# A hybrid transformer block on one core: the sums of Strassen products continued in a PSUM bank, and twenty splits moved from GpSimd to VectorE

## The chip, the cores and the metric

The kernel runs on one core of a Trainium2 chip. The metric is the device time of one execution in microseconds. The engines are called as in the profile: PE is TensorE's matmul, DVE is VectorE, ACT is ScalarE, POOL is GpSimd, SP is SyncE, which here issues DMAs. PSUM is the memory that PE writes; a bank holds 128 x 512 float32.

## The reference

One block over x of 1024 rows by 1024 columns. What the change touches is the projection into q, k and the gates, and the first matmul of the feed-forward part:

```python
h_in = rms_norm(x, norm_mix_g[l], NORM_EPS)
proj = h_in @ w_in[l]
qa, ka, va, qb, kb, vb, ga, gb = jnp.split(proj, split_idx, axis=-1)
...
merged = jax.nn.sigmoid(ga) * ya + jax.nn.sigmoid(gb) * yb
x = x + merged @ w_out[l]
h2 = rms_norm(x, norm_mlp_g[l], NORM_EPS)
x = x + jnp.square(jax.nn.relu(h2 @ w_ff1[l])) @ w_ff2[l]
return rms_norm(x, norm_final_g, NORM_EPS)
```

Between the two stand a windowed attention with three dilations and a differential attention, each with rotary positions on q and k.

## The kernel before

The program is one straight list of instructions, written as Python with tiles taken from pools. A scheduler puts it into an order for each engine; on the chip each engine then works through its own queue in that order, and semaphores make it wait for others. A tile's tag has a number of buffers ("slots"), and a new tile of the tag must wait until the readers of the tile that had its slot before are done.

The execution has five stages: norm and v (0 to 144 us), q, k and gates (144 to 426 us), attention, the branch outputs, the output projection and the early part of ff1 (426 to 1057 us), ff1 (1057 to 1327 us) and ff2 (1327 to 1700 us).

In the second and fourth stage a block of 256 output columns, a *pair*, is computed as two halves by the seven products of Strassen and Winograd. There are 8 q/k pairs, 8 gate pairs and 16 ff1 pairs. The transposed activations lie ready as seven operands named B11, B21, B22, T1, T2, T3 and T4. A product (L242) is twelve matmuls of 128 x 128 by 128 x 512: four steps of K by three terms, since each float32 operand is split into a high part (`_h`, written by ACT) and a low part (`_l`, the rest, a subtraction on POOL or DVE). The split is `halves` (L248); its tiles `wh` and `wl` have three slots each.

Of each pair come these steps. `col_raw` loads two tiles of weights, `w_n0` and `w_n1`, 512 KB each, by SP; raw tiles have two slots for each of two turns, so that the load for a pair takes the slot of the pair two before. `rest_operands` (L270) makes four sums on DVE: `s` (L273), and in place a21 (L274), a11 (L275) and a12 (L276); then the splits `ws` (of a11 and a12, for T2 and B22), `wd` (of `s`, for T1) and `wt` (of a21 and a22, for T3 and T4). `ws` and `wt` are split by POOL, 128 x 1024 each, `wd` by DVE. `rest_products` (L282) issues the five products T2, B22, T1, T3 and T4 into five banks: two double banks with the tag S (names `y...` and `z...`) and one with the tag T (`4...`), all with two slots. Six sums on DVE make the blocks c12, c22 and c21 out of the banks. The pair's other two products, B11 and B21, give `p1` and c11 in `first_products` (L262); `w1a` and `wa` are the splits for them.

These two come at different times. Four of the q/k pairs (EARLY) and seven of the ff1 pairs have p1 beforehand; the other four q/k pairs and ff1 pairs 7 to 13 compute it in their own turn, so they have seven products; the gates and ff1 pairs 14 and 15 leave it out here (`p1 is None`) and add it later. So the second stage has 88 products and the fourth 94. The order of the ff1 pairs is 6, 0, 1, 2, 3, 4, 5, 7 and up. In the second stage q/k pairs and gates alternate, and each q/k pair is followed by its rotary step (`rope`, L496 to L515): four DMAs, one multiplication on POOL (L503), three instructions on DVE (L502, L504, L513) of 128 x 1024, and one on ACT.

In the functions below `done` stores a finished block; in ff1 ACT first squares it (`squared`, L1140).

Of the kernel before, what the change touches and what calls it, by code (L numbers as in the profile page):

```python
# [19 lines left out]
P = 128  # L20
# [63 lines left out]
def tile_hybrid_block(ctx: ExitStack, tc: tile.TileContext, t: dict, out: bass.AP):  # L84
    nc = tc.nc
# [15 lines left out]
    def bank(shape, tag, name):  # L101
        return psum["ps"].tile(shape, F32, tag=tag, name=name, bufs=psum["bufs"][tag])
# [21 lines left out]
    def bank2(name):  # L124
        return bank([P, 1024], "S", name)
# [78 lines left out]
    DK = DC // 2  # L204
    hb = {}
# [33 lines left out]
            nc.scalar.activation(hi[:, :, c], x, AF.Copy)  # L239
            eng.tensor_tensor(lo[:, :, c], x, f(hi[:, :, c]), op=ALU.subtract)  # L240

    def product(acc, w, nm):  # L242
        for k in range(DK):
            for wz, hz in ((0, 0), (0, 1), (1, 0)):
                nc.tensor.matmul(acc, w[wz][:, k, :], hb[nm][hz][:, k, :], start=k == 0 and wz + hz == 0,  # L245
                                 stop=k == DK - 1 and wz == 1)

    def halves(x, name, eng=nc.gpsimd):  # L248

        hi = wp.tile([P, DC, P], F32R, tag="wh", name=name + "_h", bufs=3)  # L250
# [11 lines left out]
    def first_products(name, a11, a12, p1, c11, tags=("mm", "gm")):  # L262

        acc = [bank([P, 512], tag, f"f{z}{name}") for z, tag in enumerate(tags)]
        product(acc[0], a11, "B11")
        nc.scalar.activation(p1, acc[0], AF.Copy)
        product(acc[1], a12, "B21")
        nc.vector.tensor_tensor(c11, acc[1], p1, op=ALU.add)

    def rest_operands(name, ra, rb, s1):  # L270

        a11, a12, a21, a22 = ra[:, :DK, :], ra[:, DK:, :], rb[:, :DK, :], rb[:, DK:, :]
        nc.vector.tensor_tensor(s1, a21, a22, op=ALU.add)  # L273
        nc.vector.tensor_tensor(a21, a11, a21, op=ALU.subtract)  # L274
        nc.vector.tensor_tensor(a11, s1, a11, op=ALU.subtract)  # L275
        nc.vector.tensor_tensor(a12, a12, a11, op=ALU.subtract)  # L276
        s2, s4 = halves(ra, f"ws_{name}")
        (s1,) = halves(s1, f"wd_{name}", nc.vector)
        s3, a4 = halves(rb, f"wt_{name}")
        return s1, s2, s3, s4, a4  # L280

    def rest_products(name, operands, p1, u, dst, done):  # L282

        s1, s2, s3, s4, a4 = operands
        acc2 = bank2(f"y{name}")
        b6, b3 = acc2[:, 0:512], acc2[:, 512:1024]
        acc2 = bank2(f"z{name}")
        b5, b7 = acc2[:, 0:512], acc2[:, 512:1024]
        b4 = bank([P, 512], "T", f"4{name}")
        c12, c21, c22 = dst  # L290
        product(b6, s2, "T2")
        product(b3, s4, "B22")
        if p1 is None:
            nc.scalar.activation(u, b6, AF.Copy)
        else:
            nc.vector.tensor_tensor(u, b6, p1, op=ALU.add)
        nc.vector.tensor_tensor(c12, b3, u, op=ALU.add)
# [12 lines left out]
    act0 = tc.tile_pool(name="act0", bufs=1)  # L310
# [6 lines left out]
    s1 = tc.tile_pool(name="s1", bufs=1, side="right")  # L317
# [118 lines left out]
    def s1_tile(name):  # L436
        return p1.tile([P, DK, P], F32, tag="s1", name=f"s1_{name}", bufs=2)
# [87 lines left out]

    def qk_pair(j, raws):
        xa, xb = [big("x", f"raw{j + a}", 4) for a in range(2)]
        p, u = [p1.tile([P, 512], F32, tag="p1", name=f"{nm}{j}", bufs=4) for nm in ("qp", "qu")]
        if j in EARLY:
            for z, x in enumerate((p, xa[:, 0:512])):  # L530
                nc.sync.dma_start(x, early_d[EARLY.index(j)][z])
        else:
            a11, a12 = halves(raws[0], f"wa_q{j}")
            first_products(f"q{j}", a11, a12, p, xa[:, 0:512])
        operands = rest_operands(f"q{j}", *raws, s1_tile(f"q{j}"))
        rest_products(f"q{j}", operands, p, u, (xa[:, 512:], xb[:, :512], xb[:, 512:]), lambda *_: None)
# [612 lines left out]
    def ff1_first(n, r, eng, *tags):  # L1149
        a11, a12 = halves(r, f"w1a_{n}", eng)  # L1150
        p1 = p5.tile([P, 512], F32, tag="p1", name=f"p1_{n}", bufs=NEARLY)
        c11 = c_tile(f"c11_{n}")
        first_products(f"f{n}", a11, a12, p1, c11, *tags)
        squared(n, 0, 0, c11)
        return p1
# [17 lines left out]


# [41 lines left out]
    last_w = {n: col_raw(w_ff1, 256 * n, f"w1_last{n}", *SLOTS[n % 2]) for n in late}
# [186 lines left out]
```

## Time and profile before

| what | value |
|---|---|
| median of 3 runs | 1702.39 us (1696.2 to 1707.07) |
| the profiled execution | 1701.56 us |
| its span, first to last instruction | 1699.8 us |
| around the span | 1.76 us |
| mean granted clock of PE | 0.967 |
| PE busy, matmul | 1569.3 us, 92% |
| DVE busy | 1230.8 us, 72% |
| ACT busy | 709.4 us, 42% |
| POOL busy | 712.4 us, 42% |

Busy is the time in which an engine had an instruction running. A wait is named by the instruction that waited and the one whose end released it. The granted clock is a mean over a stretch, in parts of full speed. A window is a stretch of the span in us from its start.

### The profile page before, as it was taken

Reading aid. Unit: us, or ns where it says so; the run is one execution under the profiler, and the core shown is the slowest. Engines: PE = TensorE matmul, PEld = TensorE weight load, DVE = VectorE, ACT = ScalarE, POOL = GpSimd, SP = SyncE. Lnnn points to the kernel's source line nnn. Section 1 sums busy time; section 2 is a strip of 40 time slices with the busy share of each in tenths; the row PEclk is TensorE's granted clock in tenths of the full one; section 3 lists DMA queues with packets and bytes.
Section 4 is the critical chain, followed back from the end, with each engine's and each line's share of the span. In section 5 each row is a group of like instructions: output and inputs, shape, how many; then the busy total and the mean of one; then the engine's idle time right before and its main releaser. Section 6 shows DMA issues by size and latency. Waiting matters only on the chain. (4 is left out here: it accounts for less than half of the span.)

```text
span 1699.8 us, 22314 instructions
## 1 busy us (share of the span) xinstructions
PE 1569.3 (92%) x8216; PEld 1324.2 (78%) x8216; DVE 1230.8 (72%) x1560; ACT 709.4 (42%) x1176; POOL 712.4 (42%) x412
## 2 busy tenths in 40 slices
PE   7899989998889998999999998999999888999997
PEld 6798767776677778899879996777888677777776
DVE  5876788689688996555546548544344899999995
ACT  4432222222567774445422336345444643333322
POOL 1634545455223241112120016333333498888771
PEclk8999999999899998999999999999999999999999
DMA  6366576555855658665475432433332632222212
GB/s 203 130 207 211 169 227 227 166 179 175 267 192 191 230 192 276 186 203 187 144 250 184 137 96 73 147 120 115 113 112 93 248 137 99 99 100 99 87 38 99
DMA packets 211869, 272.36 MB, mean 160 GB/s; under 512 B 12304, under 2 KB 146608, under 8 KB 211760
## 3 DMA queue, kind: packets, MB, share of 16 engines
q1 hardware_dynamic: 207152, 254.16, 46.0%
q10 hardware_dynamic: 4608, 16.78, 2.5%
q8 instruction: 65, 1.06, 0.3%
q14 instruction: 44, 0.36, 0.1%
HBM read 184.86 MB, written 80.27 MB: 156 GB/s over the span
## 5 line engine op out<-in xcount | busy, mean ns | idle before, releaser
L1291 PE MATMUL p<-wb_h,fa_h 128*128 128x512 f32 x392 | 157.1, 402 | 21.5 <-DVE xb L1301 8.1
L1292 PE MATMUL p<-wb_l,fa_h 128*128 128x512 f32 x392 | 155.8, 397 | 4.2 <-DVE wb_l L1249 4.2
L1293 PE MATMUL p<-wb_h,fa_l 128*128 128x512 f32 x392 | 155.3, 397 | 0.0
L1291 PEld LDWEIGHTS p<-wb_h,fa_h 128*128 128x128 f32 x392 | 74.9, 191 | 44.4 <-issue 14.5
L1249 POOL TENSOR_TENSOR wb_l<-ws,wb_h 128x512 fp32r<-128x512 f32 x54 | 86.0, 1603 | 17.3 <-ACT wb_h L1248 17.3
L1292 PEld LDWEIGHTS p<-wb_l,fa_h 128*128 128x128 f32 x392 | 75.5, 193 | 20.7 <-DVE wb_l L1249 5.2
L1293 PEld LDWEIGHTS p<-wb_h,fa_l 128*128 128x128 f32 x392 | 75.3, 192 | 16.5 <-DVE fa_l L1249 0.5
L702 ACT ACTIVATE p<-sb,mn 128x1024 f32<-128x1024 f32 x64 | 71.4, 1117 | 38.3 <-DVE mn L700 24.1
L697 PE MATMUL sb<-kb,qb 128*128 128x512 f32 x256 | 74.7, 416 | 13.1 <-ACT p L702 7.6
L700 DVE TENSOR_REDUCE mn<-sb 128x1 f32<-128x1024 f32 x64 | 76.7, 1216 | 11.0 <-PE sb L697 10.7
L1249 POOL TENSOR_TENSOR wb_l<-w2r,wb_h 128x512 fp32r<-128x512 f32 x48 | 78.7, 1660 | 13.7 <-ACT wb_h L1248 13.7
L164 POOL TENSOR_SCALAR n_y<-n_ss 128x1 f32<-128x1 f32 x23 | 6.0, 261 | 186.1 <-ACT n_xn L171 183.1
L273 DVE TENSOR_TENSOR s<-w 128x512 f32<-128x512 f32 x15 | 13.5, 901 | 97.2 <-DMA w<-in_w_ff 97.2
L254 POOL TENSOR_TENSOR wt_f_l<-w,wt_f_h 128x1024 fp32r<-128x1024 f32 x15 | 36.1, 2408 | 91.6 <-ACT wt_f_h L253 91.6
L1248 ACT ACTIVATE fa_h<-fs 128x512 fp32r<-128x512 f32 x56 | 35.1, 627 | 84.9 <-issue 40.9
L1249 DVE TENSOR_TENSOR fa_l<-fs,fa_h 128x512 fp32r<-128x512 f32 x56 | 70.4, 1264 | 0.0
L811 PE MATMUL sa<-kh_a,zq 128*128 128x256 f32 x256 | 69.2, 301 | 0.0
L1248 ACT ACTIVATE fa_h<-fr 128x512 fp32r<-128x512 f32 x50 | 31.2, 626 | 90.7 <-PE p L1292 52.2
L836 DVE TENSOR_TENSOR pta<-ta,pta 128x512 fp32r<-128x512 f32 x64 | 43.8, 688 | 33.7 <-ACT pta L835 33.4
L697 PEld LDWEIGHTS sb<-kb,qb 128*128 128x128 f32 x256 | 46.4, 194 | 25.4 <-ACT p L702 11.2
L811 PE MATMUL sa<-kl_a,zq 128*128 128x256 f32 x256 | 66.1, 289 | 0.0
L1142 ACT ACTIVATE c<-c 128x512 f32<-128x512 f32 x64 | 39.6, 623 | 56.2 <-DVE c L300 50.1
(500 smaller groups left out, 5272.1 us busy)
## 6 DMA issues: line engine op xcount, KB each, us to landing
w<-in_w_in SPq DMA_DIRECT2D x32, 512.0 KB, 4.2
qk<-r ACTq DMA_DIRECT2D x32, 512.0 KB, 4.5
f<-c SPq DMA_DIRECT2D x64, 256.0 KB, 4.6
w2r<-in_w_ff SPq DMA_DIRECT2D x32, 512.0 KB
fr<-f SPq DMA_DIRECT2D x32, 512.0 KB, 6.2
w<-in_w_ff SPq DMA_DIRECT2D x30, 512.0 KB
vb<-vb SPq DMA_DIRECT2D x16, 512.0 KB, 6.9
rot<-raw SPq DMA_DIRECT2D x64, 128.0 KB, 3.8
```

The lines of the kernel that those rows point to most:

```text
L254: eng.tensor_tensor(lo[:, :n, :], x, f(hi[:, :n, :]), op=ALU.subtract)
L697: nc.tensor.matmul(sps[:, 512 * n:512 * n + 512], q[:, z, (qb % 4) * P:(qb % 4 + 1) * P], o.k[m][:, 512 * n:512 * n + 512], start=z == 0, ...
L700: nc.vector.tensor_reduce(mn, sps, axis=AX.X, op=ALU.min)
L702: nc.scalar.activation(p, sps, AF.Exp, scale=-1.0, bias=mn, accum_out=o.zz[qb][:, m:m + 1])
L811: nc.tensor.matmul(ps[:, 0:CM], zq[:, n % 4, c, :], kk[:, c * CM:(c + 1) * CM], start=c == 0 and kk is o.kh, stop=c == NCLS - 1 and kk is ...
L836: nc.vector.tensor_tensor(view[1], tv, f(view[0]), op=ALU.subtract)
L1142: nc.scalar.activation(c, c, AF.Relu)
L1248: nc.scalar.activation(hi, x, AF.Copy)
L1249: eng.tensor_tensor(lo, x, f(hi), op=ALU.subtract)
L1291: nc.tensor.matmul(acc, ah[:, c], bh, start=i == 0, stop=False)
L1292: nc.tensor.matmul(acc, ah[:, c], bl, start=False, stop=False)
L1293: nc.tensor.matmul(acc, al[:, c], bh, start=False, stop=i == len(ops) - 1)
```

## The change

`product` gets a flag `more`: with it the first matmul does not clear the bank, so that the product is added to what the bank holds. `rest_products` then needs one double bank, `y...`, and the banks T. Its first half, `bx`, takes T2 and then T3 on top, in pairs with their own first products B11 before them; its second half, `bz`, takes T1 and then B22 on top. What is needed in between is copied out: `u` after T2 and `w` after T3, by ACT where p1 is in the bank already or is left out (`alone`), otherwise by DVE with p1 added. Then c22 is bz + w, c21 is the bank of T4 plus w, and c12 is bz + u after B22 has been added. B22 is now the last product of a pair. The first products of a pair move into `rest_products`. The splits `wa`, `ws` and `wt` of the q/k pairs, 4 + 8 + 8 instructions, go to DVE; those of the gates and of ff1 stay on POOL. (`wh`, `wl` and the raw tiles keep their slots.)

```diff
-    def product(acc, w, nm):
+    def product(acc, w, nm, more=False):
...
-                nc.tensor.matmul(acc, w[wz][:, k, :], hb[nm][hz][:, k, :], start=k == 0 and wz + hz == 0,
-                                 stop=k == DK - 1 and wz == 1)
+                nc.tensor.matmul(acc, w[wz][:, k, :], hb[nm][hz][:, k, :], start=k == 0 and wz + hz == 0 and not more,
+                                 stop=k == DK - 1 and wz == 1, skip_group_check=more)
...
-    def rest_operands(name, ra, rb, s1):
+    def rest_operands(name, ra, rb, s1, eng=nc.gpsimd):
...
-        s2, s4 = halves(ra, f"ws_{name}")
+        s2, s4 = halves(ra, f"ws_{name}", eng)
         (s1,) = halves(s1, f"wd_{name}", nc.vector)
-        s3, a4 = halves(rb, f"wt_{name}")
+        s3, a4 = halves(rb, f"wt_{name}", eng)
...
-    def rest_products(name, operands, p1, u, dst, done):
+    def rest_products(name, operands, p1, uw, dst, done, first=None):
...
-        acc2 = bank2(f"y{name}")
-        b6, b3 = acc2[:, 0:512], acc2[:, 512:1024]
-        acc2 = bank2(f"z{name}")
-        b5, b7 = acc2[:, 0:512], acc2[:, 512:1024]
+        two = bank2(f"y{name}")
+        bx, bz = two[:, 0:512], two[:, 512:1024]
+        c12, c21, c22 = dst
+        u, w = uw
+        if first:
+            a11, a12, c11 = first
+            by = bank([P, 512], "T", f"f{name}")
+            product(bx, a11, "B11")
+            nc.scalar.activation(p1, bx, AF.Copy)
+            product(by, a12, "B21")
+            nc.vector.tensor_tensor(c11, by, p1, op=ALU.add)
+            done(0, 0, c11)
+        alone = first or p1 is None
+
+        def up_to_here(x):
+            if alone:
+                nc.scalar.activation(x, bx, AF.Copy)
+            else:
+                nc.vector.tensor_tensor(x, bx, p1, op=ALU.add)
+
+        product(bx, s2, "T2", more=bool(first))
+        up_to_here(u)
+        product(bz, s1, "T1")
+        product(bx, s3, "T3", more=True)
+        up_to_here(w)
+        nc.vector.tensor_tensor(c22, bz, w, op=ALU.add)
+        done(1, 1, c22)
         b4 = bank([P, 512], "T", f"4{name}")
-        c12, c21, c22 = dst
-        product(b6, s2, "T2")
-        product(b3, s4, "B22")
-        if p1 is None:
-            nc.scalar.activation(u, b6, AF.Copy)
-        else:
-            nc.vector.tensor_tensor(u, b6, p1, op=ALU.add)
-        nc.vector.tensor_tensor(c12, b3, u, op=ALU.add)
-        product(b5, s1, "T1")
-        product(b7, s3, "T3")
-        nc.vector.tensor_tensor(c12, b5, c12, op=ALU.add)
+        product(b4, a4, "T4")
+        nc.vector.tensor_tensor(c21, b4, w, op=ALU.add)
+        done(1, 0, c21)
+        product(bz, s4, "B22", more=True)
+        nc.vector.tensor_tensor(c12, bz, u, op=ALU.add)
         done(0, 1, c12)
-        nc.vector.tensor_tensor(c21, b7, u, op=ALU.add)
-        nc.vector.tensor_tensor(c22, b5, c21, op=ALU.add)
-        done(1, 1, c22)
-        product(b4, a4, "T4")
-        nc.vector.tensor_tensor(c21, b4, c21, op=ALU.add)
-        done(1, 0, c21)
...
-            a11, a12 = halves(raws[0], f"wa_q{j}")
-            first_products(f"q{j}", a11, a12, p, xa[:, 0:512])
-        operands = rest_operands(f"q{j}", *raws, s1_tile(f"q{j}"))
-        rest_products(f"q{j}", operands, p, u, (xa[:, 512:], xb[:, :512], xb[:, 512:]), lambda *_: None)
+            first = (*halves(raws[0], f"wa_q{j}", nc.vector), xa[:, 0:512])
+        operands = rest_operands(f"q{j}", *raws, s1_tile(f"q{j}"), nc.vector)
+        rest_products(f"q{j}", operands, p, (u, w), (xa[:, 512:], xb[:, :512], xb[:, 512:]), lambda *_: None, first)
```

The scheduler puts the new program into an order of its own. The line numbers in the rows of the changed program are its own, 1 higher at `halves` (L255) and in the four sums (L274 to L277); `u` and `w` are written at L304 by ACT or L306 by DVE, c22 at L313, c21 at L317, c12 at L320.

First place: DVE in ff1, pair 2. `s_4`, `w_41` and `w_40` belong to pair 4, the pair after next; `wd_f_l` is a split of the pair after this one. Before:

```order
L296 TENSOR_TENSOR u_10227<-yf_10231,p_2_9626 128x512 [waits PE_49]
L273 TENSOR_TENSOR s_4_10412<-w_41_10328 128x512 [waits DMAHW1_49]
L297 TENSOR_TENSOR c_2_10228<-yf_10231,u_10227 128x512 [waits DMAHW5_49,DVE_49]
L274 TENSOR_TENSOR w_41_10328<-w_40_10326,w_41_10328 128x512 [waits DMAHW6_49,DVE_49,Pool_49]
L275 TENSOR_TENSOR w_40_10326<-s_4_10412,w_40_10326 128x512 [waits DVE_49]
L254 TENSOR_TENSOR wd_f_l<-s_3_10309,wd_f_h 128x512 [waits PE_49,Activation_49]
L276 TENSOR_TENSOR w_40_10326<-w_40_10326 128x512 [waits DVE_49]
L300 TENSOR_TENSOR c_2_10228<-zf_10232,c_2_10228 128x512 [waits PE_49]
L302 TENSOR_TENSOR c_2_10229<-zf_10232,u_10227 128x512 [waits DMAHW7_49]
L303 TENSOR_TENSOR c_2_10230<-zf_10232,c_2_10229 128x512 [waits DMAHW0_49,DVE_49]
L306 TENSOR_TENSOR c_2_10229<-4f_10233,c_2_10229 128x512 [waits DVE_49,PE_49]
```

and now:

```order
L306 TENSOR_TENSOR u_10204<-yf_10209,p_2_9606 128x512 [waits DVE_49,PE_49]
L274 TENSOR_TENSOR s_4_10387<-w_41_10304 128x512 [waits DMAHW1_49,DVE_49]
L275 TENSOR_TENSOR w_41_10304<-w_40_10302,w_41_10304 128x512 [waits DMAHW6_49,DVE_49,Pool_49]
L276 TENSOR_TENSOR w_40_10302<-s_4_10387,w_40_10302 128x512 [waits DVE_49]
L277 TENSOR_TENSOR w_40_10302<-w_40_10302 128x512 [waits DVE_49]
L306 TENSOR_TENSOR w_10205<-yf_10209,p_2_9606 128x512 [waits PE_49]
L313 TENSOR_TENSOR c_2_10208<-yf_10209,w_10205 128x512 [waits DMAHW5_49,DVE_49]
L317 TENSOR_TENSOR c_2_10207<-4f_10252,w_10205 128x512 [waits DMAHW7_49,PE_49]
L255 TENSOR_TENSOR wd_f_l<-s_3_10285,wd_f_h 128x512 [waits Activation_49]
L320 TENSOR_TENSOR c_2_10206<-yf_10209,u_10204 128x512 [waits DMAHW0_49,PE_49]
```

Before, the sums of pair 4 (L273 to L276) lay among those of pair 2, with one of pair 2 (L297) second behind `s_4`. Now all four stand in one piece behind `u`, and `w`, c22, c21 and c12 of pair 2 come behind them.

Second place: PE in ff1, pair 2, at the start of B22. `yf` is the double bank of the pair, `4f` the bank of T4. Before, where T2 ends:

```order
L245 MATMUL yf_10231<-hT_9445,ws_f_h 128x512
L245 MATMUL yf_10231<-hT_9444,ws_f_l 128x512
L245 MATMUL yf_10231<-hB_9440,ws_f_h 128x512
L245 MATMUL yf_10231<-hB_9441,ws_f_h 128x512
L245 MATMUL yf_10231<-hB_9440,ws_f_l 128x512
L245 MATMUL yf_10231<-hB_9440,ws_f_h 128x512
```

and now, where T3 ends and the last eight matmuls of T4 follow:

```order
L246 MATMUL yf_10209<-hT_9427,wt_f_h 128x512
L246 MATMUL yf_10209<-hT_9426,wt_f_l 128x512
L246 MATMUL 4f_10252<-hT_9429,wt_f_h 128x512
L246 MATMUL 4f_10252<-hT_9428,wt_f_l 128x512
L246 MATMUL 4f_10252<-hT_9428,wt_f_h 128x512
L246 MATMUL 4f_10252<-hT_9429,wt_f_h 128x512
L246 MATMUL 4f_10252<-hT_9428,wt_f_l 128x512
L246 MATMUL 4f_10252<-hT_9428,wt_f_h 128x512
L246 MATMUL 4f_10252<-hT_9429,wt_f_h 128x512
L246 MATMUL 4f_10252<-hT_9428,wt_f_l 128x512
L246 MATMUL yf_10209<-hB_9420,ws_f_h 128x512 [waits DVE_49]
L246 MATMUL yf_10209<-hB_9421,ws_f_h 128x512
```

B22 (the operand `hB`) followed T2 in a bank half of its own. Now it is the pair's last product, and its first matmul waits for DVE.

Third place: DVE in the q/k stage, behind the second q pair (`qu`, `qw`, `raw`), with the gate that follows it (`gc`). `s_g` and `w_5...` are of the next gate, `ws_q` and `wt_q` are splits of the next q pair. Before:

```order
L306 TENSOR_TENSOR raw_1719<-4q_1743,raw_1719 128x512 [waits DVE_49,PE_49]
L276 TENSOR_TENSOR w_40_1810<-w_40_1810 128x512 [waits DVE_49]
L273 TENSOR_TENSOR s_g_2039<-w_51_1909 128x512 [waits DMAHW7_49]
L297 TENSOR_TENSOR gc_1815<-yg_1835,gu_1814 128x512 [waits DMAHW6_49,Activation_49]
L274 TENSOR_TENSOR w_51_1909<-w_50_1907,w_51_1909 128x512 [waits DMAHW1_49,DVE_49,Pool_49]
L275 TENSOR_TENSOR w_50_1907<-s_g_2039,w_50_1907 128x512 [waits DVE_49]
L254 TENSOR_TENSOR wd_q_l<-s_q_1945,wd_q_h 128x512 [waits PE_49,Activation_49]
L276 TENSOR_TENSOR w_50_1907<-w_50_1907 128x512 [waits DVE_49]
```

and now:

```order
L320 TENSOR_TENSOR raw_1716<-yq_1740,qu_1719 128x512 [waits PE_49]
L255 TENSOR_TENSOR ws_q_l<-w_40_1807,ws_q_h 128x1024 [waits PE_49,Activation_49]
L274 TENSOR_TENSOR s_g_2035<-w_51_1905 128x512 [waits DMAHW1_49]
L275 TENSOR_TENSOR w_51_1905<-w_50_1903,w_51_1905 128x512 [waits DMAHW6_49,DVE_49,Pool_49]
L313 TENSOR_TENSOR gc_1815<-yg_1833,gw_1812 128x512 [waits Activation_49]
L276 TENSOR_TENSOR w_50_1903<-s_g_2035,w_50_1903 128x512 [waits DVE_49]
L277 TENSOR_TENSOR w_50_1903<-w_50_1903 128x512 [waits DVE_49]
L317 TENSOR_TENSOR gc_1814<-4g_1874,gw_1812 128x512 [waits PE_49]
L255 TENSOR_TENSOR wd_q_l<-s_q_1942,wd_q_h 128x512 [waits Activation_49]
L320 TENSOR_TENSOR gc_1813<-yg_1833,gu_1811 128x512 [waits DMAHW5_49,PE_49]
```

The split `ws_q` of the next q pair, 128 x 1024, stands on DVE between the last sum of the q pair and `s_g` of the next gate, and the first sum of the gate's blocks (L313) comes behind `s_g` and a21.

## Rows read from the trace of the kernel before

**Rows 1.** The windows by stage: window, length, each engine's busy us (instructions), clock.

```profile
144.00:426.00 282.00, 259.63 (x1058) 202.30 (x1058) 229.12 (x216) 71.17 (x81) 140.15 (x52) 0.96 0.62 195
...
1057.00:1327.00 270.00, 263.88 (x1140) 215.08 (x1141) 127.16 (x182) 113.46 (x168) 96.64 (x41) 0.99 0.37 114
```

**Rows 2.** The windows, four shorter stretches of the same two stages.

```profile
186.00:200.00 14.00, 14.00 (x55) 11.21 (x54) 9.64 (x12) 2.65 (x3) 4.13 (x2) 0.89 0.67 213
392.00:406.00 14.00, 8.83 (x30) 6.29 (x29) 13.93 (x13) 3.05 (x5) 4.84 (x2) 0.76 0.53 154
1085.00:1100.00 15.00, 13.83 (x62) 11.15 (x61) 7.66 (x12) 6.11 (x9) 4.20 (x3) 1.00 0.41 135
1155.00:1175.00 20.00, 20.00 (x89) 16.40 (x88) 7.39 (x12) 9.62 (x15) 8.37 (x5) 1.00 0.39 118
```

**Rows 3.** The waits of PE from 144 to 426 us: us in total, times, longest.

```profile
PE zg L245 <- DVE raw L303: 5.8, 4, 4.1
PE zq L245 <- DVE gc L303: 4.4, 2, 3.6
```

**Rows 4.** The waits of PE from 1057 to 1327 us, the largest.

```profile
PE yf L245 <- DVE c L297: 3.8, 5, 1.2
```

**Rows 5.** The waits of DVE from 1057 to 1327 us, the largest.

```profile
DVE s L273 <- DMA w<-in_w_ff: 97.2, 14, 7.7
```

**Rows 6.** The timeline of ff1, 1096 to 1140 us: start, length, engine, line.

```profile
1096.44 0.69 DVE L296 TENSOR_TENSOR u<-yf,p 128x512 f32<-128x512 f32 x1 [1.24 <-PE yf L245]
...
1109.74 1.04 ACT L253 ACTIVATE wt_f_h<-w 128x1024 fp32r<-128x1024 f32 x1
...
1110.87 2.41 POOL L254 TENSOR_TENSOR wt_f_l<-w,wt_f_h 128x1024 fp32r<-128x1024 f32 x1 [9.70 <-ACT wt_f_h L253]
...
1113.30 0.38 SPq L259 DMA_DIRECT2D w<-in_w_ff  x1
...
1113.52 2.40 POOL L254 TENSOR_TENSOR ws_f_l<-w,ws_f_h 128x1024 fp32r<-128x1024 f32 x1 [0.24 <-ACT ws_f_h L253]
...
1118.22 0.69 DVE L273 TENSOR_TENSOR s<-w 128x512 f32<-128x512 f32 x1 [6.94 <-DMA w<-in_w_ff]
...
1119.43 0.68 DVE L274 TENSOR_TENSOR w<-w,w 128x512 f32<-128x512 f32 x1
...
1120.14 0.69 DVE L275 TENSOR_TENSOR w<-s,w 128x512 f32<-128x512 f32 x1
...
1139.81 0.69 DVE L296 TENSOR_TENSOR u<-yf,p 128x512 f32<-128x512 f32 x1 [0.63 <-PE yf L245]
```

**Rows 7.** The timeline of ff1, 1186 to 1197 us.

```profile
1186.29 0.58 ACT L266 ACTIVATE p<-f0f 128x512 f32<-128x512 f32 x1
...
1188.48 2.40 POOL L254 TENSOR_TENSOR wt_f_l<-w,wt_f_h 128x1024 fp32r<-128x1024 f32 x1 [3.54 <-ACT wt_f_h L253]
...
1190.91 0.38 SPq L259 DMA_DIRECT2D w<-in_w_ff  x1
...
1193.96 2.40 POOL L254 TENSOR_TENSOR w1a_l<-w,w1a_h 128x1024 fp32r<-128x1024 f32 x1 [3.08 <-ACT w1a_h L253]
...
1195.53 1.37 DVE L273 TENSOR_TENSOR s<-w 128x512 f32<-128x512 f32 x1 [7.25 <-DMA w<-in_w_ff]
```

**Rows 8.** The timeline of q/k and gates, 204 to 210 us.

```profile
204.09 2.40 POOL L503 TENSOR_TENSOR raw<-raw,cos_t 128x1024 f32<-128x1024 f32 x1 [0.46 <-DMA rot<-raw]
204.10 0.68 DVE L297 TENSOR_TENSOR gc<-yg,gu 128x512 f32<-128x512 f32 x1
...
204.71 2.33 DVE L274 TENSOR_TENSOR w<-w,w 128x512 f32<-128x512 f32 x1
...
208.88 1.22 DVE L502 SCALAR_TENSOR_TENSOR rot<-rot,sin_t 128x1024 f32<-128x1024 f32 x1
```

**Rows 9.** The groups of instructions from 144 to 426 us: count, busy us, mean ns.

```profile
L504 DVE SCALAR_TENSOR_TENSOR raw<-raw,rot 128x1024 f32<-128x1024 f32 x16 | 35.1, 2194 | 2.7 <-POOL raw L503 2.3
...
L274 DVE TENSOR_TENSOR w<-w,w 128x512 f32<-128x512 f32 x14 | 20.4, 1455 | 0.6
```

More of the change, by code (lines that the diff above doesn't have):

```diff
@@ L527, in qk_pair @@
         xa, xb = [big("x", f"raw{j + a}", 4) for a in range(2)]
-        p, u = [p1.tile([P, 512], F32, tag="p1", name=f"{nm}{j}", bufs=4) for nm in ("qp", "qu")]
+        p, u, w = [p1.tile([P, 512], F32, tag="p1", name=f"{nm}{j}", bufs=4) for nm in ("qp", "qu", "qw")]
         if j in EARLY:
+            first = None
             for z, x in enumerate((p, xa[:, 0:512])):
@@ L542, in gate_rest @@
     def gate_rest(n, raws):
-        u = p1.tile([P, 512], F32, tag="p1", name=f"gu{n}", bufs=4)
+        uw = [p1.tile([P, 512], F32, tag="p1", name=f"{nm}{n}", bufs=4) for nm in ("gu", "gw")]
         dst = [p1.tile([P, 512], F32, tag="x", name=f"gc{n}{k}", bufs=4) for k in range(3)]
@@ L547, in done @@
             nc.sync.dma_start(part_d[n][2 * a + b - 1], c)
-        rest_products(f"g{n}", rest_operands(f"g{n}", *raws, s1_tile(f"g{n}")), None, u, dst, done)
+        rest_products(f"g{n}", rest_operands(f"g{n}", *raws, s1_tile(f"g{n}")), None, uw, dst, done)
     GATES = (4, 5, 6, 7, 0, 1, 2, 3)
@@ L1162, in ff1_operands, with ff1_rest @@
         return rest_operands(f"f{n}", ra, rb, s1)
-    def ff1_rest(n, operands, p1):
-        u = p5.tile([P, 512], F32, tag="u", name=f"u_{n}", bufs=2)
+    def ff1_rest(n, operands, p1, first=None):
+        uw = [p5.tile([P, 512], F32, tag="u", name=f"{nm}_{n}", bufs=2) for nm in "uw"]
         if n == NP2 - NLATE and NLATE > 1:
@@ L1169, in ff1_rest @@
             dst = [c_tile(f"c{nm}_{n}") for nm in ("12", "21", "22")]
+        if first:
+            p1 = p5.tile([P, 512], F32, tag="p1", name=f"p1_{n}", bufs=NEARLY)
+            first = (*first, c_tile(f"c11_{n}"))
         late = []
-        rest_products(f"f{n}", operands, p1, u, dst, (lambda *x: late.append(x)) if p1 is None else partial(squared, n))
+        rest_products(f"f{n}", operands, p1, uw, dst, (lambda *x: late.append(x)) if p1 is None else partial(squared, n), first)
         return late
@@ L1206, in tile_hybrid_block @@
             cur = raws
-            if n < NP2 - NLATE and n not in first:
-                first[n] = ff1_first(n, cur[0], nc.gpsimd)
+            both = halves(cur[0], f"w1a_{n}", nc.gpsimd) if n < NP2 - NLATE and n not in first else None
             operands = ff1_operands(n, *cur)
@@ L1212, in tile_hybrid_block @@
         if n < NP2 - NLATE:
-            ff1_rest(n, operands, first.pop(n))
+            ff1_rest(n, operands, first.pop(n, None), both if i else None)
         else:
```

## The prediction

> **What bounds the kernel now.** I read the windows by stage first. The change touches two stages of five: the q/k projections with the gates (144 to 426 us) and ff1 (1057 to 1327 us) [rows 1]. In both PE is the fullest engine: 259.63 of 282.00 us in the first, so 22.4 us are idle, and 263.88 of 270.00 us in the second, so 6.1 us are idle. The second view cuts ff1 finer [rows 2]: from 1155 to 1175 us PE never stops, 89 matmuls in 20.00 us, so one product of twelve matmuls takes 12 x 20.00 / 89 = 2.70 us. A us that PE loses here is a us of the end, since the next stage starts from the last of these products; a us that DVE, ACT or POOL save is worth only what PE waits less. So the third view is the waits of PE [rows 3, 4]: ff1 loses 3.8 us to the add `c12=b3+u`, and q/k loses 5.8 and 4.4 us to L303. The fourth is the wait of DVE in ff1: 97.2 us in 14 waits for the raw weights of a later pair [rows 5]. That wait is harmless in the kernel before: every PSUM pair is double buffered, and PE has other banks to write while the batch of adds that stands behind the load is late. The rows show this: DVE stands still for 6.94 us up to 1118.22 us [rows 6] while a pair's period is (1139.81 - 1096.44) / 3 = 14.46 us [rows 6], against 5 x 2.70 = 13.5 us of matmuls.
>
> **The change, what it saves.** No matmul goes. Of adds on DVE one goes from each pair with a ready p1, three from one with its own first product, two from one without p1; they take 0.68 us each [rows 6]. In ff1 DVE is busy for 127.16 of 270 us [rows 1], so nothing there was bound by it, and the 0.58 us that ACT needs for a copy [rows 7] is hidden under the next product. I put this at nothing in ff1; its cover is DVE's own idle time, and without that cover it would be worth 0.68 us for each add. In q/k, where DVE is busy for 229.12 of 282 us, 32 adds go (4 x 1 + 4 x 3 + 8 x 2), 21.8 us, and 20 splits come, 20 x 1.22 = 24.4 us by the DVE instruction of the same size [rows 8]. POOL loses those 20, 20 x 2.40 = 48 us. DVE stays as full as it was; POOL gets emptier.
>
> **The change, what it adds.** B22 is now computed last, on top of T1 in the same bank, and so it may start only after `c22 = bz + w` has read that bank. The order of PE shows the wait on DVE at the first of its matmuls. In front of `w` and `c22` the order of DVE has the four adds of the pair after next, of which the first waits for the load. A wait that cost nothing is now in the chain of PE. Its price for ff1 pairs 0 to 5, with t=0 where the former pair's B22 ends:
> - The slots of the split weights are three deep and `wt` takes the one that B22 of the former pair frees. So ACT's `wt` hi runs from 0.25 to 1.3 (1.04 us [rows 6], started 0.25 us after its releaser, as POOL is at 1113.52 [rows 6]), POOL's lo to 3.8 (2.40 us [rows 6]).
> - The load of the pair after next takes the raw tile that this lo has read: in the rows, lo ends at 1110.87 + 2.41 = 1113.28, the load is issued at 1113.30 and `s` starts at 1118.22 [rows 6], so 4.94 us after lo. That is t=8.75.
> - Then `s`, `a21`, `a11`, `a12`, `w`, `c22` follow, six dependent adds at 0.70 (1119.43 to 1120.14 is the step of two of them [rows 6]): c22 ends at 12.95, B22 starts at 13.05, and the period is 13.05 + 2.70 = 15.75, 1.3 us over 14.46.
> - POOL may make it worse. The hi of the next pair's `ws` may start when T1 ends, t=7.05, so POOL's lo lies at 8.4 to 10.8, across `s`. An add with two SBUF inputs that meets a POOL instruction ends about 0.55 us after it: `s` at 1195.53 took 1.37 us instead of 0.69 while POOL ran from 1193.96 to 1196.36 [rows 7], and L274 at 204.71 took 2.33 us while POOL ran from 204.09 to 206.49; L297 at 204.10, which reads PSUM, took 0.68 us through the same [rows 8]. So `s` ends at 11.35, c22 at 14.6, B22 starts at 14.7, and the period is 17.4, which is 2.95 over before.
> - PE itself would be through its other products at T2 2.7, four matmuls of T4 with a wait of 0.6 for `wt` lo 4.3, T1 7.05, T3 9.77, the rest of T4 11.6. So it stands for 1.4 us in the one case, 3.1 in the other.
>
> [...]
>
> Pairs 7 to 13, with t=0 where B21 ends: `wt` lo ends at 3.75, `s` may start 4.65 us later (1188.48 + 2.40 = 1190.88 to 1195.53 [rows 7]), at 8.4; POOL's `w1a` lo of the next pair lies at 8.1 to 10.5 across it; c22 ends at 13.65 by the blocked count, at 11.75 without. PE has B22 due at 11.4, or 10.85 had it not waited 0.55 for `wt` lo. So 2.9 us for each pair, at least 0.8. From 1155 to 1175 us, among these pairs, PE had no idle time at all [rows 2].
>
> The sum for ff1: pairs 0 to 3, 4 x 2.95 = 11.8; pair 4, which has two adds less in front, 1.7; pair 5 2.95; pair 6, where the adds of two pairs stand ahead of `w`, 3.0; pairs 7 to 13, 7 x 2.9 = 20.3 and 1.3 more in pair 12, which has two further adds; pairs 14 and 15 nothing, since no load is ahead of them. That is 41 us. With nothing blocked it is 4 x 1.3 + 0.3 + 1.3 + 2.0 + 7 x 0.8 = 14.4; with pair 6 at 5 us and 0.2 more in each other it is 46. I take 41, since rows 7 show a POOL lo across `s` in the same place already.
>
> q/k and gates: the new wait is there as well. In a gate `c22` stands behind the split of the next q's `ws` and the `s` of the next gate, whose load is issued when POOL has done `wt` of this gate. From the end of q's B22: 3.7 for `wt`, 4.9 for the load, 0.25, three adds of 0.70, 10.85 to 11; PE has until then the rest of T2 0.6, T1, T3 and T4, 8.7. So 2.15 us for each of 8 gates, 17. For the q pairs I bound it by the waits of the same bank hand-over before: L303 cost 5.8 / 4 = 1.45 us a time and at most 4.1 [rows 3]. Their load is issued earlier than before, since its releaser is now a split of 1.22 us and not of 2.40, so I take the low end, 8 x 1.45 = 12. Together 29 against the 22.4 us idle now, most of which are waits at L297, L303 and the splits that the new order replaces: +6 us. Bounds: q at nothing and the gates at 13, -9; q at 4.1 each, 33 + 17 - 22 = +28, cut to +24 since the fewer POOL instructions block less.
>
> **The sum.** The profiled execution took 1701.56 us (a span of 1699.8 and 1.76 around it), 0.8 below the median of the three runs, 1702.39. 1701.6 + 41 + 6 = 1749 us. With the bounds: 1701.6 + 14 - 9 = 1707 and 1701.6 + 46 + 24 = 1772.
>
> **Rivals.**
> - *Relief, the other side.* In q/k, DVE lost time to POOL: 16 instructions L504 at 2.194 us instead of 1.22 and 14 of L274 at 1.455 instead of 0.69 [rows 9], 15.6 + 10.7 us. 20 of POOL's 52 instructions go, and with fewer blocks the 22.4 us idle might go nearly whole. In ff1 this needs B22 to be free of `s`: c22 must be done by 11.6, so `s` must start by 7.4, so the load must land 3.6 us after its issue and not 4.9. From there it decides. Then ff1 is level and the time 1702 - 22 = 1680 to 1690 us. Against it speaks that all loads before `s` in ff1 took 4.6 to 4.9 us.
> [...]
> - *Unblocked.* The chain through the load is there but POOL's instructions miss `s`: 1701.6 + 14 + 4 = 1720 us.
> - *Nothing.* The scheduler's order is the same in effect, since the wait of DVE is taken up by ACT's copies and T4's matmuls: 1702 us. Against it: the PE instruction waits for DVE in the built program, and DVE's adds ahead of c22 wait for the load.
>
> **How the numbers follow.** The forecast (1735 to 1765) 0.45, unblocked (1708 to 1735) 0.22, clock (1765 to 1790) 0.15, nothing 0.10, relief 0.08. The range is 1708 to 1785: it leaves out most of the last two and the far end of the clock. One per cent, 17 us, is about what a measurement can tell from no change. Faster by more (below 1685) is half of relief, 0.04; within it are nothing, the other half of relief and the low third of unblocked, 0.20; slower 0.76.
>
> **What would show it.** Right: in ff1 the first matmul of B22 waits for DVE's c22 some 2 to 3 us, in nearly all pairs but the last two; DVE's wait before `s` is still there; T4's third matmul waits about 0.5 us for POOL's `wt` lo; the ff1 stage is some 40 us longer, q/k within 10 us of its 282. Wrong: PE's waits for c22 below 1 us (the load lands early), a granted clock below 0.95 in ff1 (the clock), or q/k shorter by 10 us or more (relief).

## The result, and the profile after

The changed kernel takes 1792.62 us, median of 4 runs (1789.24 to 1798.11), against 1702.14 us before: the ratio is 1.0536 with an interval of 1.0493 to 1.0579. The profiled execution has a span of 1791.4 us, 91.6 us more than before. Cut at the first instruction of each stage, the loss lies where the change is: from the first q product to the first attention score 325.6 us instead of 287.9, and from the first ff1 product to the first of ff2 340.3 instead of 278.5. The three other parts together are 7.9 us shorter. Here are the two stages in the windows, cut in this way, before (two lines) and after:

```profile
144.30:432.20 287.90, 260.13 (x1059) 202.46 (x1059) 229.17 (x215) 71.17 (x81) 140.28 (x52) 0.96 0.62 197
1057.00:1335.50 278.50, 272.38 (x1177) 221.90 (x1178) 132.24 (x191) 121.42 (x184) 96.64 (x41) 0.99 0.39 122
...
139.10:464.70 325.60, 273.96 (x1069) 208.17 (x1069) 198.97 (x204) 82.92 (x98) 92.42 (x34) 0.94 0.56 177
1083.70:1424.00 340.30, 298.50 (x1177) 233.16 (x1178) 135.08 (x159) 134.36 (x200) 96.54 (x41) 0.93 0.32 99
```

In ff1 PE now idles 340.3 - 298.5 = 41.8 us, where it was 6.1. But its busy time has grown too, by 26 us, for the same matmuls, and the granted clock fell from 0.99 to 0.93. So two things were lost: time in which PE stood, and time in which it ran slower. The waits of PE in ff1 say for what it stood:

```profile
PE yf L246 <- DVE c L313: 34.3, 14, 3.6
PE 4f L246 <- POOL wt_f_l L255: 4.5, 15, 0.5
```

Fourteen pairs wait for c22, 2.45 us each; the wait for L297 [rows 4] is gone. Two stands for c22 in the timeline of ff1, where [rows 6] showed the old order:

```profile
1161.02 0.69 DVE L313 TENSOR_TENSOR c<-yf,w 128x512 f32<-128x512 f32 x1
...
1161.77 1.22 PE L246 MATMUL yf<-hB,ws_f_h 128*128 128x512 f32 x2 [3.03 <-DVE c L313]
...
1163.21 1.05 PE L246 MATMUL yf<-hB,ws_f_h 128*128 128x512 f32 x2
...
1168.90 0.69 DVE L306 TENSOR_TENSOR u<-yf,p 128x512 f32<-128x512 f32 x1 [2.03 <-PE yf L246]
...
1169.60 0.50 PE L246 MATMUL 4f<-hT,wt_f_l 128*128 128x512 f32 x1 [0.29 <-POOL wt_f_l L255]
...
1173.93 0.69 DVE L274 TENSOR_TENSOR s<-w 128x512 f32<-128x512 f32 x1 [4.34 <-DMA w<-in_w_ff]
...
1174.12 2.76 POOL L255 TENSOR_TENSOR ws_f_l<-w,ws_f_h 128x1024 fp32r<-128x1024 f32 x1 [4.57 <-ACT ws_f_h L254]
...
1174.71 2.71 DVE L275 TENSOR_TENSOR w<-w,w 128x512 f32<-128x512 f32 x1
...
1179.51 0.69 DVE L313 TENSOR_TENSOR c<-yf,w 128x512 f32<-128x512 f32 x1
...
1180.26 0.73 PE L246 MATMUL yf<-hB,ws_f_h 128*128 128x512 f32 x2 [2.61 <-DVE c L313]
...
1181.06 0.62 PE L246 MATMUL yf<-hB,ws_f_h 128*128 128x512 f32 x2
...
1186.03 0.69 DVE L306 TENSOR_TENSOR u<-yf,p 128x512 f32<-128x512 f32 x1 [2.03 <-PE yf L246]
```

`u` to `u` is 17.13 us here, forecast 17.4; in the three pairs before, whose B22 ran slowly, it is 18.5 to 19.2. The load lands and `s` runs at 1173.93, POOL's `ws` lo runs from 1174.12 to 1176.88 and the next sum, with two SBUF inputs, ends 0.54 us after it; then the sums, `w`, c22 at 1179.51, and B22 at 1180.26 after a stand of 2.61 us. In 14 of the 15 batches of four sums in ff1 one sum is held like this and takes 2.15 to 2.80 us; in twelve of them it is `s` (shortest, median and longest in ns):

```profile
L274 DVE TENSOR_TENSOR s<-w x15: 684/2528/2800, 1095.3 to 1374.7; 128x512 f32<-128x512 f32 x15
```

At 1161.77 the stand was 3.03 us long, and behind it B22 ran slowly for 3 us (two matmuls took 1.05 us at 1163.21, against 0.62 at 1181.06). Over all pairs this is the slowness: B22 is 516 and 493 ns a matmul, where the other products have 389 to 417 (columns: busy, mean ns, idle before).

```profile
L246 PE MATMUL yf<-hB,ws_f_h 128*128 128x512 f32 x128 | 54.4, 516 | 34.3 <-DVE c L313 34.3
...
L246 PE MATMUL yf<-hB,ws_f_l 128*128 128x512 f32 x64 | 31.6, 493 | 0.0
```

That is 54.4 + 31.6 = 86.0 us; the same two groups of B22 had 39.4 and 24.9 us before, so 21.7 us more. In q/k the waits of PE are of several kinds:

```profile
PE yq L246 <- DVE qu L306: 11.4, 3, 5.6
PE yq L246 <- DVE raw L313: 8.2, 5, 3.3
PE yg L246 <- DVE gc L313: 6.9, 4, 3.3
PE sb L711 <- DMA qb<-qk: 6.5, 1, 6.5
PE yg L246 <- POOL ws_g_l L255: 5.7, 3, 2.0
```

The wait of the first score for its DMA, 6.5 us, is not new. Before it was

```profile
PE sb L697 <- DMA qb<-qk: 5.6, 1, 5.6
```

The largest wait was not forecast: the first matmul of T1 waits for `u`. The timeline of the longest, 5.59 us:

```profile
209.75 2.36 DVE L255 TENSOR_TENSOR wt_q_l<-w,wt_q_h 128x1024 fp32r<-128x1024 f32 x1 [0.17 <-ACT wt_q_h L254]
...
212.03 1.21 DVE L516 SCALAR_TENSOR_TENSOR rot<-rot,sin_t 128x1024 f32<-128x1024 f32 x1
...
213.34 1.23 DVE L518 SCALAR_TENSOR_TENSOR raw<-raw,rot 128x1024 f32<-128x1024 f32 x1
...
215.15 2.35 POOL L517 TENSOR_TENSOR raw<-raw,cos_t 128x1024 f32<-128x1024 f32 x1 [4.12 <-DMA rot<-raw]
...
215.69 2.89 DVE L527 TENSOR_TENSOR r<-raw,r 128x1024 fp32r<-128x1024 f32 x1 [1.12 <-ACT r L526]
218.50 1.21 DVE L516 SCALAR_TENSOR_TENSOR rot<-rot,sin_t 128x1024 f32<-128x1024 f32 x1
...
219.63 0.68 DVE L306 TENSOR_TENSOR qu<-yq,qp 128x512 f32<-128x512 f32 x1
...
220.36 1.22 PE L246 MATMUL yq<-hT,wd_q_h 128*128 128x512 f32 x2 [5.59 <-DVE qu L306]
```

`u` can be read when T2 is done, but ahead of it on DVE stand the split `wt` and four rope instructions (L516, L518, L527, L516). L527 took 2.89 us, beside POOL's L517, which ran from 215.15 to 217.50. The clock after it, beside three stretches of ff1 behind a stand, and two of these stands:

```profile
221.00:229.00 8.00, 8.00 (x26) 6.18 (x24) 3.67 (x6) 2.50 (x3) 0.51 (x1) 0.68 0.82 299
1161.80:1164.50 2.70, 2.70 (x7) 2.12 (x8) 1.20 (x2) 2.67 (x5) 0.00 (x0) 0.50 0.11 36
1213.80:1216.50 2.70, 2.70 (x12) 2.22 (x13) 0.50 (x1) 2.21 (x4) 2.24 (x1) 1.00 0.00 0
1237.00:1239.50 2.50, 2.50 (x7) 1.93 (x7) 0.00 (x0) 2.02 (x4) 2.07 (x1) 0.50 0.28 105
```

```profile
1213.76 0.73 PE L246 MATMUL yf<-hB,ws_f_h 128*128 128x512 f32 x2 [2.68 <-DVE c L313]
...
1235.79 0.73 PE L246 MATMUL yf<-hB,ws_f_h 128*128 128x512 f32 x2 [2.13 <-DVE c L313]
```

After the stand of 5.59 us the mean granted clock of the next 8 us was 0.68, in which PE never stopped. Behind the stand of 3.03 us it was 0.50; behind one of 2.68 us it was 1.00; and behind one of 2.13 us it fell to 0.50 a few matmuls later. So the length of these stands alone does not tell whether the clock falls. Of the fourteen stands for c22 eleven had slow matmuls behind them, five of these after 2.12 to 2.13 us each; the other three, of 1.58, 2.61 and 2.68 us, had none.

### The profile page after: what moved, and what is told of

It is laid out like the page before. It is cut to its first block, busy times and chain, and to the rows that moved or that the text cites. A ratio compares the mean times of both kernels' runs of the same rounds, so it can differ in the third digit from the quotient of the medians.

```text
span 1791.4 us, 22215 instructions
## 1 busy us (share of the span) xinstructions
PE 1603.3 (89%) x8216; PEld 1333.8 (74%) x8216; DVE 1205.5 (67%) x1516; ACT 734.2 (41%) x1208; POOL 659.0 (37%) x392
## 5 line engine op out<-in xcount | busy, mean ns | idle before, releaser
L274 DVE TENSOR_TENSOR s<-w 128x512 f32<-128x512 f32 x15 | 32.7, 2182 | 85.2 <-DMA w<-in_w_ff 85.2
L517 POOL TENSOR_TENSOR raw<-raw,cos_t 128x1024 f32<-128x1024 f32 x16 | 47.5, 2970 | 107.4 <-DMA rot<-raw 76.3
L246 PE MATMUL yf<-hB,ws_f_h 128*128 128x512 f32 x128 | 54.4, 516 | 34.3 <-DVE c L313 34.3
L1265 POOL TENSOR_TENSOR wb_l<-w2r,wb_h 128x512 fp32r<-128x512 f32 x48 | 77.7, 1637 | 17.4 <-ACT wb_h L1264 17.4
L255 POOL TENSOR_TENSOR wt_f_l<-w,wt_f_h 128x1024 fp32r<-128x1024 f32 x15 | 36.0, 2401 | 115.3 <-ACT wt_f_h L254 97.2
L850 DVE TENSOR_TENSOR pta<-ta,pta 128x512 fp32r<-128x512 f32 x64 | 43.8, 688 | 33.7 <-ACT pta L849 33.6
```

The lines of the kernel that those rows point to most:

```text
L517: nc.gpsimd.tensor_tensor(raw, raw, cos_t, op=ALU.mult)
L1265: eng.tensor_tensor(lo, x, f(hi), op=ALU.subtract)
```

## The experiments

Times are medians; ratios are to the kernel before, run on the same chip.

**One part alone, or without it** (four kernels). The first gives the kernel before the q/k splits on DVE; the second takes them back from the changed kernel; the third and fourth use the new products in one stage and the old ones in the other.

```diff
 a1_split, to the kernel before
-            a11, a12 = halves(raws[0], f"wa_q{j}")
+            a11, a12 = halves(raws[0], f"wa_q{j}", nc.vector)
-        operands = rest_operands(f"q{j}", *raws, s1_tile(f"q{j}"))
+        operands = rest_operands(f"q{j}", *raws, s1_tile(f"q{j}"), nc.vector)
 a2_sums, to the changed kernel: these two without nc.vector
 a3_ff1: qk_pair and gate_rest call the old rest_products, splits on GpSimd
 a4_qk: ff1_rest calls the old rest_products and ff1_first
```

> The kernel before with one part of the change alone: the 20 splits of the q/k pairs on VectorE. Theory (the bank hand-over to B22 is what costs): no hand-over here, so within 12 us of before, 1690 to 1714 us. Rival (VectorE is overfull in the q/k stage and the splits make the loss there): 1730 us or more, nearly all of the q/k stage's loss of 38 us.

> The changed kernel with the q/k splits back on GpSimd. Theory: the hand-over stays in both stages, the loads of a q/k pair are released 1.2 us later, 1785 to 1810 us. Rival (the splits): 1755 to 1765 us, as ff1's loss alone.

> The new products in ff1 alone; q/k pairs, gates and splits as before. Theory: ff1's loss of 62 us is its own, 1702 + 62 = 1764 us, between 1755 and 1775, with 34 us of waits for c22 and the rest by the clock after them. Rival (ff1 loses because of what the stages ahead leave behind): under 1740 us.

> The new products and splits in q/k pairs and gates alone; ff1 as before. Theory: 1702 + 30 = 1732 us, between 1722 and 1742 us, so that the two parts together make the whole. Rival: over 1745 us, if the parts help each other.

a1_split: 1693.06 us, ratio 0.9946 (0.9927 to 0.9964), half a per cent faster. In the profiled execution q/k takes 281.5 us instead of 287.9. The groups of that stage show one thing that changed: what DVE lost to POOL shrank, L504 from 2194 to 1619 ns and L274 from 1455 to 949 [rows 9]. That this makes the gain is not shown, since the splits are also shorter (`ws` 2052 ns and `wt` 1484 ns in the mean on DVE, where POOL took 2522 and 2823) and can release the loads earlier.

```profile
L504 DVE SCALAR_TENSOR_TENSOR raw<-raw,rot 128x1024 f32<-128x1024 f32 x16 | 25.9, 1619 | 0.3
...
L274 DVE TENSOR_TENSOR w<-w,w 128x512 f32<-128x512 f32 x14 | 13.3, 949 | 0.3
```

a2_sums: 1814.05, 1.0651 (1.0611 to 1.0691), 21 us worse than the change and 4 above the theory's range. a3_ff1: 1766.59, 1.0363 (1.0327 to 1.0398). a4_qk: 1728.84, 1.0137 (1.0093 to 1.0181). So the splits are a gain in either kernel, the products are the loss, and the losses add: 63.2 + 25.5 = 88.7 of 90.5 us. In a4_qk the first score comes after 322.7 us, as in the whole change, and ff1 is back at 277.8.

**The hand-over to B22.** b1_own_bank gives B22 a bank of its own and c12 one more add; b5_order_ff1 leaves the banks and only has DVE's four sums issued behind c22 of the pair two before; b6_order does so in both stages.

```diff
 b1_own_bank, to the changed kernel
-        product(bz, s4, "B22", more=True)
         nc.vector.tensor_tensor(c12, bz, u, op=ALU.add)
+        b3 = bank1(f"3{name}")
+        product(b3, s4, "B22")
+        nc.vector.tensor_tensor(c12, b3, c12, op=ALU.add)
 b5_order_ff1 (ff1 alone) and b6_order
-        nc.vector.tensor_tensor(c22, bz, w, op=ALU.add)
+        c22s.append(nc.vector.tensor_tensor(c22, bz, w, op=ALU.add).ins)
...
+        with tc.issue_after(c22s[-2]):
             nc.vector.tensor_tensor(s1, a21, a22, op=ALU.add)
             ...
```

> The changed kernel, but B22 goes into a bank of its own and one more add on VectorE puts it to c12; so no matmul waits for c22, while T3 still goes on top of T2. Theory (B22 waits for c22 to have read its bank): the waits for c22 vanish in both stages and the clock in ff1 comes back, 1700 to 1725 us. Rival (going on in a bank, or the later place of B22 with the slots of its split weights, is what costs): 1760 us or more.

> The changed kernel, with VectorE's four weight sums of the pair after next issued behind c22 in ff1 alone; nothing else in the order moves and the hand-over to B22 stays. Theory (c22 is late because sums that wait for a load stand ahead of it): c22 is done when PE gets to B22, ff1 loses only the 0.5 us per pair at T4, 1792 - 52 = 1740 us, between 1732 and 1750. Rival (the hand-over itself, T3 to w to c22 to B22, takes too long): 1775 us or more.

> As the run with the sums behind c22, but in q/k pairs and gates too. Theory: q/k loses its 15 us of waits for c22 and some of the clock, the waits of T1 for u stay at 11 us, 1720 to 1738 us. Rival (in q/k the chain from the load to the next pair's splits is as critical as c22): 1742 us or more, as with ff1 alone.

b5_order_ff1: 1745.98 us, 1.0257 (1.0235 to 1.0279), as the theory had it. PE's order in ff1 is the same but for three matmuls near its start; ff1 takes 293.5 us instead of 340.3, and PE's waits there are

```profile
PE yf L246 <- DVE c L318: 6.9, 7, 1.4
PE 4f L246 <- POOL wt_f_l L255: 5.4, 16, 0.7
```

with a granted clock of 0.99. b6_order: 1735.32, 1.0179 (1.0136 to 1.0223): q/k falls from 325.6 to 306.7 us, c22's waits there from 15.1 to 6.0, while T1's waits for `u` stay (14.5 us). b1_own_bank: 1743.77, 1.0242 (1.0226 to 1.0258), a miss by 19 us. PE waits for c22 in neither stage any more, but ff1 still takes 306.5 us at a granted clock of 0.96, since PE stands for T4's weights instead:

```profile
PE 4f L246 <- POOL wt_f_l L255: 12.3, 15, 1.8
PE 4f L246 <- ACT wt_f_h L254: 6.2, 4, 3.0
```

These are 18.5 us, 13.7 of them in the pairs 0 to 4. One place of the timeline there, with the last matmul of a B22 (into `3f`) and what ACT does after it:

```profile
1155.78 0.39 PE L246 MATMUL 3f<-hB,ws_f_l 128*128 128x512 f32 x1
...
1156.46 0.63 ACT L1158 ACTIVATE c<-c 128x512 f32<-128x512 f32 x1 [6.68 <-DVE c L313]
...
1159.23 1.04 ACT L254 ACTIVATE wt_f_h<-w 128x1024 fp32r<-128x1024 f32 x1
```

B22 ends at 1156.17, and with it the use of the slot that `wt` takes, but ACT splits `wt` only 3.06 us later. It works without a stop in between, on a row of instructions that begins with the squaring of c22 (L1158), for which it had waited 6.68 us. In all five of these pairs `wt` starts 1.2 to 4.6 us after B22's end, behind such a row. So c22 was still late, and its lateness reached PE through ACT's queue instead of through the bank.

**GpSimd in the chain.** b2_dve_ff1 puts ff1's splits on DVE too.

```diff
-        return rest_operands(f"f{n}", ra, rb, s1)
+        return rest_operands(f"f{n}", ra, rb, s1, nc.vector)
...
-            both = halves(cur[0], f"w1a_{n}", nc.gpsimd) if ...
+            both = halves(cur[0], f"w1a_{n}", nc.vector) if ...
```

> The changed kernel with ff1's splits on VectorE too, so that GpSimd does nothing in ff1. Theory: the low part of wt is ready at 2.6 instead of 3.8 us, the load comes 1.2 us earlier, no GpSimd instruction holds the sums, c22 comes at 11.3 to 12.3 where PE needs it at 11 to 11.6: ff1 loses at most 1 us per pair, 1735 to 1755 us. Rival (the chain is bound by the load, whoever splits): 1775 us or more.

1737.53 us, 1.0199 (1.0175 to 1.0223). ff1 takes 285.1 us, though `s` and a21 still stand ahead of c22. PE's waits for it there are

```profile
PE yf L246 <- DVE c L313: 4.2, 10, 1.2
```

So POOL's 2.40 us, once in the chain and once across the sums, were most of ff1's wait; this run takes away both and does not tell them apart.

**The clock.** b4_fill puts eight needless matmuls into an unused bank ahead of each B22 of ff1.

```diff
+            junk = bank1(f"j{name}")
+            for k in range(8):
+                nc.tensor.matmul(junk, s4[0][:, k % DK, :], hb["B22"][0][:, k % DK, :], start=k == 0, stop=k == 7)
         product(bz, s4, "B22", more=True)
```

> The changed kernel with 8 needless matmuls (1.8 us) into an unused bank before each B22 of ff1. Theory (after the stand of 2.45 us the granted clock is low and B22's matmuls take 0.51 us instead of 0.39, 23 us in all): the stand shrinks to 0.6 us, the matmuls of B22 are at 0.39 again, and more work makes the kernel faster, 1765 to 1778 us. Rival (B22 is slow since it adds to a bank that an engine has just read): B22 stays at 0.5 us, 1790 us or more.

1783.15 us, 1.0475 (1.0456 to 1.0494): 9.5 us less than the changed kernel with 128 matmuls more, where 15 to 28 were expected. All four executions (1776.35 to 1784.01) lie below all four of the changed kernel (1789.24 to 1798.11). The groups and the window of ff1, from the fastest of the four:

```profile
L246 PE MATMUL yf<-hB,ws_f_h 128*128 128x512 f32 x128 | 42.3, 412 | 12.5 <-DVE c L313 12.5
```

```profile
1082.90:1411.10 328.20, 310.27 (x1304) 245.35 (x1305) 137.55 (x159) 133.40 (x200) 96.77 (x41) 0.98 0.33 103
```

B22 is at 412 ns instead of 516, and the granted clock at 0.98. The 128 matmuls are 128 x 20.00 / 89 = 28.8 us of the 310.27 busy [rows 2], the rest 281.5, 17.0 less than in the changed kernel. So no cost of adding to a bank that was just read shows here: with 12.5 us of stands for c22 in ff1 instead of 34.3, B22 lies within the 389 to 417 ns that the other products had in the changed kernel. In this execution, 1776.35 us, the time is within the forecast; the median is 5 us above it, and what the slower three lost is not shown.

**The shared tile.** c1_two_tiles makes bz a tile of its own; c3_all adds the order of b6_order and the splits of b2_dve_ff1 to that; c4_splits is the kernel before with the splits of q/k and ff1 on DVE.

```diff
 c1_two_tiles, c3_all
-        bx, bz = two[:, 0:512], two[:, 512:1024]
+        bx, bz = two[:, 0:512], bank1(f"z{name}")
 c4_splits, to a1_split
-        return rest_operands(f"f{n}", ra, rb, s1)
+        return rest_operands(f"f{n}", ra, rb, s1, nc.vector)
-                first[n] = ff1_first(n, cur[0], nc.gpsimd)
+                first[n] = ff1_first(n, cur[0], nc.vector)
```

> The changed kernel with bz as a tile of its own (the free single banks) and not as the other half of bx's tile; T3 and B22 still go on top of T2 and T1. In the changed kernel the first matmul of T1 waits for u although u reads the other bank of the tile. Theory (that wait, 11 us in q/k where rope stands ahead of u on VectorE, is made by the shared tile): the waits of T1 for u vanish, PE issues T1 right behind T2, q/k is 12 to 25 us shorter, ff1 15 to 30 us, 1740 to 1765 us; the waits of B22 for c22 stay in part. Rival (T1 is late because of its operands): 1780 us or more.

> The products of the change with three repairs: bz in a tile of its own, the weight sums behind c22 in both stages, ff1's splits on VectorE. Theory: no hand-over wait is left, so the change costs nothing in ff1 (within 4 us of 278.5) and q/k is near that of the splits alone (281.5), 1690 to 1712 us. Rival (seven banks in place of ten bound the products themselves): 1720 us or more.

> The kernel before with the splits of q/k pairs and of ff1 on VectorE; the products as before. Theory: ff1 has 4.4 us of waits at the add after B22, which GpSimd's instructions held up, so 1688 to 1694 us, the best of all. Rival: 1693 us or more, as with the q/k splits alone, or slower since wt's split now waits in VectorE's queue.

c1_two_tiles: 1744.54, 1.0246 (1.0218 to 1.0275). PE issues T1 right behind T2, earlier than in the changed kernel. q/k takes 304.0 us and ff1 308.3, 32 less than there, where 15 to 30 were forecast; how much of this is the tile's and how much the new order's is not told apart. In the waits of q/k T1 (into `zq`), though earlier, no longer waits for `u`, so the shared tile made that wait; T3 (into `yq`) does, half as long, and some of the time has moved to c22:

```profile
PE zq L246 <- DVE raw L313: 11.8, 5, 3.7
PE yq L246 <- DVE qu L306: 5.5, 2, 3.5
```

c3_all: 1690.76, 0.9948 (0.9910 to 0.9987). Both stages in the windows, q/k 285.7 us and ff1 274.7:

```profile
139.70:425.40 285.70, 262.31 (x1068) 205.13 (x1068) 208.34 (x204) 82.78 (x98) 92.64 (x34) 0.96 0.64 201
1044.60:1319.30 274.70, 270.80 (x1176) 222.10 (x1177) 154.31 (x202) 136.85 (x200) 3.07 (x2) 0.99 0.40 123
```

c4_splits: 1686.12, 0.9903 (0.9876 to 0.9930), the lowest median of all and 2 us below the theory's range, with 281.9 and 273.2 us:

```profile
138.90:420.80 281.90, 257.33 (x1060) 202.67 (x1060) 236.53 (x234) 71.11 (x81) 90.55 (x33) 0.97 0.63 200
1044.80:1318.00 273.20, 270.32 (x1176) 222.03 (x1177) 169.94 (x233) 125.06 (x185) 3.07 (x2) 0.99 0.40 124
```

Between these two the intervals overlap; the new products, repaired, are level with the old ones, not better. What gains is the move of the splits; whether by their shorter time, the earlier loads or the sums that POOL no longer holds was not taken apart.

## Why the prediction was wrong

The direction was right, and so was the mechanism in ff1: B22 waits for c22, c22 for sums that wait for a load, and a wait that nobody minded moved into PE's chain. The range (1708 to 1785) was missed by 8 us, the time by 44. Two steps of the sum failed: the clock, left out of the 41 us of ff1, and the +6 us of q/k and gates. The miss would have been larger had the three other parts not come out 7.9 us shorter, which is luck. Point by point:

- *ff1, the chain:* right. 17.13 us against 17.4 in a pair whose B22 was not slowed; PE's new idle time in ff1 is 41.8 - 6.1 = 35.7 us against a term of 41. With POOL across the sums was the right one of the two counts (one sum is held in 14 of 15 batches, and b2_dve_ff1, which takes POOL out of the sums and out of the chain, loses 30 us of the waits), and the place of the sums is what makes the wait (b5_order_ff1). A sum of 0.69 us took 2.71 us beside POOL's `ws` lo and ended 0.54 us after it, where I had counted 0.55.
- *T4:* right in kind, the third matmul waits for POOL's lo, 4.5 us in 15 waits, 0.3 us each and not 0.55. That a late c22 can also reach T4, by way of the squares ahead of the split on ACT (b1_own_bank), I had not followed up.
- *The clock:* this step failed. I gave it a chance of its own beside the forecast, 0.15, though stands of PE of 1.4 to 3.1 us are in the forecast itself. It is a term of the same sum: 26 us of busy time in ff1, of which b4_fill gives back 17. An estimate from [rows 2], 14.00 / 55 = 0.2545 us a matmul from 186 to 200 us against 20.00 / 89 = 0.2247, is 94 x 12 x 0.0298 = 33.6 us with all of ff1's products so slow, 17 with half of them and 28 with five in six. With 17 to 28 the ff1 sum is 58 to 69, and 61.8 was measured. The sign that I had named for it, a granted clock below 0.95 in ff1, came: 0.93. That the size fits is partly luck: the estimate prices whole pairs, while 21.7 of the 26 us lie in B22 alone, behind the stand, and behind eleven stands of fourteen, five of these of 2.12 to 2.13 us.
- *q/k and gates:* this term failed, +6 against +37.7. PE idles 51.6 us of 325.6, where it was 27.8 of 287.9, and its busy time is up by 13.8 us. The waits for c22 were 15.1 us where I had 29, and they did take the place of old ones (L303 and L297, 13.9 us in all). What I counted as idle time to be replaced, 22.4 us, held other waits too, and three things were in the sum at nothing: T1's wait for `u` (11.4 us, from the shared tile and from rope ahead of `u` on DVE; with two tiles T1 no longer waits for `u`, and T3's wait is 5.5), PE's waits for the split weights, which grew from 8.1 to 18.0 us and which no run took apart, and again the clock.
- *The splits:* right that POOL would be emptier, wrong that DVE would stay as full (199 us busy in q/k, after 229) and wrong to count no gain: alone they take 10 us off.
- *Relief, unblocked, nothing:* none came. The load was never early enough: `s` ran 3.9 to 5.3 us after its load was issued, and 3.6 was the bound. The first half of relief, a shorter q/k in which DVE loses less beside POOL, is what a1_split shows by itself (281.5 us instead of 287.9, L504 at 1619 ns instead of 2194).

What stays open: q/k begins 5.2 us earlier after the change, as in every variant, and the stages between are some us shorter; none of the runs was made to tell why.

## What to carry to other kernels

Adding to a PSUM bank saves additions on another engine (DVE had 32 instructions less in ff1, ACT 16 more), but it turns the read in between into a condition for the next product. Before doing it, look at what stands on the reading engine's queue ahead of that read, above all instructions that wait for a load, and at whether a wait for one half of a tile holds work on the other half. Giving the product a bank of its own is only half a cure while the late result still holds another engine's queue. And where a change makes TensorE stand again and again, the price of a lower clock after such stands belongs in the same sum, not beside it: here 26 us of busy time, with a granted clock of 0.93 in ff1 instead of 0.99.

## What the runs showed of the hardware

Needless matmuls in the gap made the kernel faster (9.5 us with 28.8 us of work added). The granted clock behind a stand of 3.03 us was 0.50 for 3.0 us (from 1161.77), behind one of 2.61 us in the next pair 1.00 (the 4 us from 1180.26), and behind five stands of 2.12 to 2.13 us 0.50 again, from a few matmuls on. With 20 subtractions of 128 x 1024 moved from POOL (2522 to 2823 ns in the means of the three groups) to DVE, other DVE instructions of the stage became faster as well, L504 by 26% (2194 to 1619 ns, a1_split).
